# Where x's transposed blocks wait for their store: in the tiles of v's quadrants, in eight pieces, instead of in operand slots

## The chip, the cores and the metric

The kernel runs on one core of one Trainium2 chip. The metric is the device time of one execution in microseconds (us). A core has TensorE (PE, with its weight loads as PEld), VectorE (DVE), ScalarE (ACT), GpSimd (POOL) and SyncE (SP), which issues all DMAs of this kernel. Each engine works through its own queue in order and waits on semaphores for the others.

## What is computed

One decoder block on x of 1024 tokens by 1024 features, in float32. The start, with which this case deals, is a normalization of x, its projection by `w_in`, and beside it the keys and values of a memory of 256 tokens:

```python
h = h + hybrid_mixer(rmsnorm(h, norm_mix[i]), w_in[i], ...)
h = h + mem_cross_attention(rmsnorm(h, norm_xattn[i]), rmsnorm(mem, norm_mem[i]), w_xq[i], w_xkv[i], w_xo[i])
h = h + swiglu(rmsnorm(h, norm_ffn[i]), w_ffn_in[i], w_ffn_out[i])
return rmsnorm(h, norm_final)
```

`hybrid_mixer` projects to z, x/B/C, dt, q, k, v, r, a1 and two gates, runs a state space branch and a gated linear attention branch, and merges them. `mem_cross_attention` takes `k, v = split(m @ w_xkv, 2)`.

## The kernel before

**Products.** A large product is done by a scheme of Strassen's kind: seven half-sized products (`CHAIN`: B11, B21, T1, B22, T2, T3, T4) instead of eight. One factor's seven operands are sums and differences of the blocks of x; `Operands` builds them from `hb`, the normalized, transposed x. To keep float32 precision every operand is split in a high and a low part (`B11h`, `B11l`, ...), and weights likewise (`whi`, `wlo`); each product is three matmuls. The splits are a copy on ScalarE (L223) and a subtraction on VectorE or GpSimd (L73, `either()` picks by a running estimate when the program is built).

**Operand slots.** The pool "op" has 14 slots of 8 KB a partition. Its first users are the memory (`mt`), x (`xt`, four), the weights for keys and values (`raw`, eight in turn), the memory's two halves (`mh`, `ml`), four tiles `xs`, and then the operands, two slots each. A slot is taken again when its user before has been read for the last time.

**The start of the program.** `x_steps()` goes over two halves `j` of the tokens and eight blocks `k` of the features: TensorE transposes a block into a PSUM bank, VectorE scales it into `hb[k]` (named `hs` in the profile), ScalarE copies it unscaled into `xs` (L608), and after four blocks SP stores 1 MB to `xT_d` (L610). `xT_d` is read again only late, for the residual. `kv_unit()` does the memory's keys and values in eight units of 256 columns; each loads 1 MB (`raw`, L513), splits it, does its matmuls and stores the result (`vm_d` or `kT_d`). `v_steps()` computes v by the seven products with 264 columns each (256 of v and 8 of a small projection): the first product goes to the quadrant tile `vq10`, the second to `vq00`, the third to `vq11`, the fourth to `vq01`; `vsa` holds a sum of the weights' quadrants. These tiles are `[P, 4, 264]`, one buffer each. PSUM has four `bank` and four `acc` tiles; both the transposes and the later units of `kv_unit` use `bank`.

**What sets the order.** The program is written as interleaved generators, and a scheduler then orders each engine's queue by readiness and priority; when a tile is free is part of readiness. SP's DMAs go through one queue with eight semaphores in rotation, so each issue also waits for the DMA issued eight before it.

**The constants.** Among SP's loads at about 34 us stand `dcol` (two loads of single elements of 4 bytes), `dtb` and `alog`.

Of the kernel before, what the change touches and what calls it, by code (L numbers as in the profile page):

```python
# [9 lines left out]
F32 = mybir.dt.float32  # L10
F32R = mybir.dt.float32r
I32 = mybir.dt.int32
AF = mybir.ActivationFunctionType
# [3 lines left out]
P = 128  # L17
# [3 lines left out]
HALF = TOK // 2  # L21
# [57 lines left out]
def block_kernel(ctx: ExitStack, tc: tile.TileContext, t: dict, out: bass.AP):  # L79
    nc = tc.nc  # L80
    now = [0.0]
    PE, ACT, SP = Tensor(nc.tensor, now), nc.scalar, nc.sync
# [7 lines left out]
    def pool(name, bufs=1, space=None, stack=None):  # L90
        kw = {"reuse_waits": "tile"} if space is None else {"space": space}
        return (stack or ctx).enter_context(tc.tile_pool(name=name, bufs=bufs, **kw))
# [6 lines left out]
    def dram(name, *shape):  # L99
        return dr.tile(list(shape), F32, name=name, tag=name)  # L100

    xT_d = dram("xT_d", D, TOK)
# [22 lines left out]
    def bank(dt=F32):  # L125
        return ps.tile([P, 512], dt, name="bank", tag="bank", bufs=4)
# [6 lines left out]
    half = lambda j: slice(j * HALF, (j + 1) * HALF)  # L133
# [8 lines left out]
    def slot(key, shape=(P, 2, TOK), dt=F32, name="sl"):  # L142
        pl, n = slots[key]
        return pl.tile(list(shape), dt, name=name, tag="sl", bufs=n)
# [6 lines left out]
    vp = pool("vp", 1, stack=st1)  # L151
# [40 lines left out]
    def col(name, i=0):  # L192
        which, at = gcol[name]
        return cols[:, which, at + i:at + i + 1]
# [12 lines left out]
    def rsqrt(o, v, scale):  # L207

        DVE.tensor_scalar(o, v, scale, EPS, ALU.mult, ALU.add)
        POOL.tensor_tensor(o, o, mhalf[:, :o.shape[1]], ALU.pow)  # L210
# [3 lines left out]
    def spread(p, r, n):  # L214

        for c in range(n):
            d = diag[c % 2]
            DVE.tensor_scalar(d, ident, r[:, c:c + 1], None, ALU.mult)
            PE.matmul(p[:, c * P:(c + 1) * P], ones, d, start=True, stop=True)
# [319 lines left out]
    for k in range(NB):  # L539
        p = bank()  # L540
# [9 lines left out]
    def kv_unit(c0):  # L550
# [32 lines left out]
        else:  # L583
            SP.dma_start(vm_d[:, c0 - D:c0 - D + 256].rearrange("(i p) c -> p i c", p=P), s)

    def x_steps():
        p = bank()
        spread(p, mss, 2)
        DVE.tensor_copy(mbc, p[:, :MEM])
        yield  # L590
        for j in range(2):
            for c in range(4 * j, 4 * j + 4):
                ACT.activation(msq, wide(xt[c // 2][:, c % 2]), AF.Square, accum_out=xr[:, c:c + 1])
            rsqrt(xr[:, 4 * j:4 * j + 4], xr[:, 4 * j:4 * j + 4], 1.0 / D)
            yield
            p = bank()
            spread(p, xr[:, 4 * j:4 * j + 4], 4)
            ACT.activation(rbc[:, half(j)], p, AF.Copy)
            yield
            for k in range(NB):  # L600
                if k % 4 == 0:
                    xs = slot("op", (P, 4, HALF), name="xs")
                p = bank()
                for a in range(4):
                    c = 4 * j + a
                    PE.transpose(p[:, a * P:(a + 1) * P], xt[c // 2][:, c % 2, k * P:(k + 1) * P], ident)
                DVE.scalar_tensor_tensor(hb[k][:, half(j)], p, col("norm_mix", k), rbc[:, half(j)], ALU.mult, ALU.mult)
                ACT.activation(xs[:, k % 4], p, AF.Copy)  # L608
                if k % 4 == 3:
                    SP.dma_start(xT_d[(k - 3) * P:(k + 1) * P, half(j)].rearrange("(k p) s -> p k s", p=P), xs)  # L610
                yield

    B = Operands(hb, 4)
# [4 lines left out]

    dt_t = cp.tile([P, NCH, NH], F32, name="dt_t")
    a1_t = cp.tile([P, NCH, NH], F32, name="a1_t")  # L620
    HW = 264

    vraw = {}

    def load_v(pr):
        if pr not in vraw:
            rr = vraw[pr] = [vp.tile([P, 4, 2 * HW], F32, name="vraw", tag=f"vraw{h}") for h in range(2)]
            for i in range(2):
                v0 = V0 + 512 * pr + 256 * i
                a0 = (DT0, A0)[pr] + 8 * i  # L630
                for h in range(2):
                    for c0, n, o in ((v0, 256, i * HW), (a0, 8, i * HW + 256)):
                        SP.dma_start(rr[h][:, :, o:o + n],
                                     w_in[512 * h:512 * h + 512, c0:c0 + n].rearrange("(k p) c -> p k c", p=P))
        return vraw[pr]

    def v_steps():
        for pr in range(2):
            rr = load_v(pr)
            A11, A21 = rr[0][:, :, :HW], rr[0][:, :, HW:]  # L640
            A12, A22 = rr[1][:, :, :HW], rr[1][:, :, HW:]
            s = {ij: vp.tile([P, 4, HW], F32, name="vq", tag=f"vq{ij[0]}{ij[1]}") for ij in
                 ((0, 0), (0, 1), (1, 0), (1, 1))}
# [6 lines left out]

            sa = vp.tile([P, 4, HW], F32, name="vsa", tag="vsa")
            for n, name in enumerate(CHAIN):
# [42 lines left out]

    kvg = chain(kv_unit(c) for c in kv_cols)
    xg = x_steps()
    load_v(0)
    for n in range(12):
# [681 lines left out]
    for n in range(len(at) + 2):  # L1381
        a = at[n] if n < len(at) else None
        b = at[n - 1] if 0 < n <= len(at) else None
# [208 lines left out]
    for x, (n, k, kn) in enumerate(todo):  # L1592
        name = CHAIN[n]
# [58 lines left out]
```

## Time and profile before

| | |
|---|---|
| median of 3 runs | 2020.72 us (2018.88 to 2021.11) |
| the profiled execution | 2022.57 us |
| its span | 2020.5 us |
| granted TensorE clock, mean | 0.992 |
| TensorE busy | 1953.7 us, 97% |
| VectorE, ScalarE, GpSimd busy | 1313.8, 860.8, 656.3 us |
| DMA | 309.58 MB, 153 GB/s over the span |

Times in the profile are in us from the start of the span. In a list of waits a row names who waits, for whom, the total, the number of waits and the longest. In a timeline a row gives start, duration, engine, line, operation, `out<-in`, tile sizes and count; in brackets at its end stands the idle time before it and what ended that. A matmul's duration overlaps the next one's, so the pace is read from the starts.

### The profile page before, as it was taken

The numbers are of one execution on the slowest core, as the hardware profiler recorded it, in microseconds if no ns is written. First come the engines' busy times: TensorE is split into PE (matmuls) and PEld (weight loads), VectorE is DVE, ScalarE is ACT, GpSimd is POOL, SyncE is SP. The second block draws the span as 40 slices with busy tenths as digits, with TensorE's granted clock in tenths as the row PEclk, the third lists the DMA queues.
The fourth block names the chain that finished last, engine by engine and source line by source line (L and its number), as shares of the span: only waits on it lengthen the run. The fifth ranks groups of instructions, "written<-read, shape, count | busy, mean of one in ns | idle before, by whom it ended". The sixth has DMA issues, their size and how long they took to land.

```text
span 2020.5 us, 26310 instructions
## 1 busy us (share of the span) xinstructions
PE 1953.7 (97%) x9772; PEld 1620.7 (80%) x9772; DVE 1313.8 (65%) x1869; ACT 860.8 (43%) x1482; POOL 656.3 (32%) x480
## 2 busy tenths in 40 slices
PE   7899899999999989999999999999999999999998
PEld 7899678877777777787788888877888888887887
DVE  6856679979886656532454227478777777774565
ACT  7434745465552455432233226453333333354243
POOL 4421243455653212023322100255444444430002
PEclk9899999999999999999999999999999999999999
DMA  7532233356553655797773210433224223276463
GB/s 247 194 117 88 94 124 116 113 181 190 168 173 110 208 163 177 244 357 244 289 237 132 80 42 22 139 124 108 79 89 134 90 82 114 77 259 218 152 227 129
DMA packets 241635, 309.58 MB, mean 153 GB/s; under 512 B 17354, under 2 KB 165044, under 8 KB 241508
## 3 DMA queue, kind: packets, MB, share of 16 engines
q1 hardware_dynamic: 241508, 307.91, 45.2%
q8 instruction: 77, 1.26, 0.3%
q14 instruction: 50, 0.41, 0.1%
HBM read 211.07 MB, written 96.80 MB: 152 GB/s over the span
## 4 chain that ended last, share of the span: by engine, by line
PE 46%; DVE 3%; DMA 2%; issue 1%; POOL 1%; ACT 1%; SPq 0%; POOLq 0%; ACTq 0%; DVEq 0%
PE acc L51 41%; PE bank L51 4%; DMA gates<-gg_d 1%; DMA fr<-act_d 1%; DVE fs L73 1%; PE bank L55 1%; POOL ssum L73 0%; POOL pre L73 0%; DMA pre<-in_w_ffn_out_dram 0%; DMA down_d<-pre 0%; DMA ysg_d<-gates 0%; DVE o L73 0%; DVE wlo L73 0%; DVE T2l L73 0%; DVE T4l L73 0%
## 5 line engine op out<-in xcount | busy, mean ns | idle before, releaser
L51 PE MATMUL acc<-hl,wd 128*128 128x512 f32 x1920 | 443.4, 391 | 6.0 <-DVE wd L73 2.9
L51 PEld LDWEIGHTS acc<-hl,wd 128*128 128x128 f32 x1920 | 360.4, 188 | 84.9 <-DVE wd L73 5.5
L73 DVE TENSOR_TENSOR wlo<-raw,whi 128x512 fp32r<-128x512 f32 x264 | 243.2, 925 | 77.1 <-ACT whi L223 76.8
L223 ACT ACTIVATE whi<-raw 128x512 fp32r<-128x512 f32 x272 | 170.2, 629 | 253.1 <-PE acc L51 224.8
L73 DVE TENSOR_TENSOR o<-acc,o 128x512 f32<-128x512 f32 (+1 forms) x256 | 172.5, 675 | 112.9 <-PE acc L51 100.6
L51 PE MATMUL acc<-fs 128*128 128x512 f32 (+1 forms) x792 | 156.0, 356 | 1.6 <-ACT o L1547 1.5
L51 PEld LDWEIGHTS acc<-fs 128*128 128x128 f32 x792 | 130.6, 189 | 22.7 <-ACT o L1547 1.9
L73 POOL TENSOR_TENSOR raw<-raw,sa 128x512 f32<-128x512 f32 x48 | 65.3, 1361 | 252.8 <-DVE wlo L73 247.1
L223 ACT ACTIVATE fs<-fr 128x1024 fp32r<-128x1024 f32 (+1 forms) x84 | 80.0, 984 | 112.7 <-PE acc L51 38.5
L73 DVE TENSOR_TENSOR fs<-fr,fs 128x1024 fp32r<-128x1024 f32 (+1 forms) x84 | 99.8, 1218 | 38.7 <-ACT fs L223 38.1
L73 DVE TENSOR_TENSOR wd<-raw,wd 128x1024 fp32r<-128x1024 f32 x40 | 50.3, 1260 | 83.1 <-ACT wd L223 82.9
L223 ACT ACTIVATE whi<-sa 128x512 fp32r<-128x512 f32 x96 | 60.0, 626 | 103.5 <-PE acc L51 103.4
L73 POOL TENSOR_TENSOR sa<-raw 128x512 f32<-128x512 f32 x47 | 74.0, 1575 | 86.2 <-DMA raw<-in_w_in_dram 47.7
L73 DVE TENSOR_TENSOR wlo<-sa,whi 128x512 fp32r<-128x512 f32 x96 | 82.6, 861 | 22.8 <-ACT whi L223 21.3
L73 POOL TENSOR_TENSOR raw<-raw 128x512 f32<-128x512 f32 x48 | 81.6, 1702 | 4.9 <-DVE sa L73 4.9
L73 POOL TENSOR_TENSOR ssum<-ssum,sq 128x512 f32<-128x512 f32 (+1 forms) x23 | 35.2, 1531 | 146.9 <-ACT sq L490 143.0
L51 PE MATMUL acc<-B21h,whi 128*128 128x512 f32 x192 | 76.9, 401 | 3.1 <-ACT o L353 3.1
L51 PE MATMUL acc<-T1h,whi 128*128 128x512 f32 x192 | 76.7, 399 | 2.7 <-ACT whi L223 2.7
L73 POOL TENSOR_TENSOR o<-o 128x512 f32<-128x512 f32 x29 | 49.2, 1703 | 91.1 <-DVE o L73 80.8
L51 PE MATMUL acc<-B21h,wlo 128*128 128x512 f32 x192 | 76.3, 398 | 2.5 <-DVE wlo L73 2.5
L51 PE MATMUL acc<-T1h,wlo 128*128 128x512 f32 x192 | 77.4, 403 | 0.5 <-DVE wlo L73 0.5
L51 PE MATMUL acc<-B22h,wlo 128*128 128x512 f32 x192 | 77.5, 404 | 0.0
(375 smaller groups left out, 4801.5 us busy)
## 6 DMA issues: line engine op xcount, KB each, us to landing
raw<-in_w_in_dram SPq DMA_DIRECT2D x26, 1024.0 KB, 5.7
raw<-in_w_ffn_in_dram SPq DMA_DIRECT2D x22, 1024.0 KB, 6.3
act_d<-o SPq DMA_DIRECT2D x77, 256.0 KB, 2.1
fr<-act_d SPq DMA_DIRECT2D x35, 512.0 KB, 6.8
pre<-in_w_ffn_out_dram SPq DMA_DIRECT2D x11, 1024.0 KB, 8.6
fr<-down_d SPq DMA_DIRECT2D x20, 512.0 KB, 3.7
down_d<-pre SPq DMA_DIRECT2D x33, 256.0 KB, 3.4
raw<-in_w_xkv_dram SPq DMA_DIRECT2D x8, 1024.0 KB, 11.4
```

What stands on the lines that cost most here:

```text
L51: return s.e.matmul(o, x, y, **kw)
L55: return s.e.transpose(o, x, i)
L73: return f(*a, **kw)
L223: ACT.activation(hi, src, AF.Copy)
```

## The change

The four tiles `xs` of four blocks leave the pool "op". Each block pair of x is copied into one of the tiles that v uses later (`XS_HOME`: first half vq10, vq00, vq11, vq01; second half vsa, vq00, vq11, vq01) and stored by itself: eight stores of 512 KB instead of four of 1 MB. The tiles vq00, vq11 and vq01 are used twice in turn, and after that all five go to v.

```diff
+    HW = 264
+
+    XS_HOME = ("vq10", "vq00", "vq11", "vq01", "vsa", "vq00", "vq11", "vq01")
+
     def x_steps():
...
             for k in range(NB):
-                if k % 4 == 0:
-                    xs = slot("op", (P, 4, HALF), name="xs")
+                if k % 2 == 0:
+                    xs = vp.tile([P, 4, HW], F32, name="xs", tag=XS_HOME[4 * j + k // 2])
+                    xs = xs.rearrange("p a b -> p (a b)")[:, :2 * HALF].rearrange("p (k s) -> p k s", k=2)
                 p = bank()
...
-                ACT.activation(xs[:, k % 4], p, AF.Copy)
-                if k % 4 == 3:
-                    SP.dma_start(xT_d[(k - 3) * P:(k + 1) * P, half(j)].rearrange("(k p) s -> p k s", p=P), xs)
+                ACT.activation(xs[:, k % 2], p, AF.Copy)
+                if k % 2:
+                    SP.dma_start(xT_d[(k - 1) * P:(k + 1) * P, half(j)].rearrange("(k p) s -> p k s", p=P), xs)
                 yield
```

The instructions on each engine stay the same in number, but for four more stores. Their order differs in the first part of the program, up to the product T1 of v, and in a few swaps of loads much later.

ScalarE before, from the split of B21's high parts on; a wait on `DMAHW` is one for a DMA, here for the store that frees T1h's slot:

```order
L223 ACTIVATE B21h<-hs 128x512 x4
L608 ACTIVATE xs<-bank 128x512 [waits DVE_49]
L223 ACTIVATE T1h<-hs 128x512 [waits DMAHW2_49,Pool_49]
L223 ACTIVATE T1h<-hs 128x512 [waits Pool_49]
L608 ACTIVATE xs<-bank 128x512 [waits DVE_49]
L684 ACTIVATE vq<-acc 128x264 [waits PE_49]
L223 ACTIVATE T1h<-hs 128x512 [waits Pool_49]
L684 ACTIVATE vq<-acc 128x264 [waits PE_49]
L608 ACTIVATE xs<-bank 128x512 [waits DVE_49]
```

ScalarE now, at the same work; the DMA waits here are for the first, second and third piece (and behind these rows comes one for the fourth):

```order
L223 ACTIVATE T1h<-hs 128x512 [waits Pool_49] x2
L687 ACTIVATE vq<-acc 128x264 [waits DMAHW3_49]
L687 ACTIVATE vq<-acc 128x264 x2
L687 ACTIVATE vq<-acc 128x264 [waits PE_49]
L223 ACTIVATE T1h<-hs 128x512 [waits Pool_49]
L613 ACTIVATE xs<-bank 128x512 [waits DMAHW4_49,DVE_49]
L613 ACTIVATE xs<-bank 128x512 [waits DVE_49]
L223 ACTIVATE T1h<-hs 128x512 [waits Pool_49]
L223 ACTIVATE B22h<-hs 128x512 [waits DVE_49,PE_49]
L223 ACTIVATE B22h<-hs 128x512 [waits DVE_49] x2
L613 ACTIVATE xs<-bank 128x512 [waits DMAHW6_49,Activation_49]
L613 ACTIVATE xs<-bank 128x512
```

The wait has moved from T1h to the copies of x and of v's first product, and B11h and B21h stand some rows further ahead.

SP before, from the fourth load of weights for the memory (the first row) to the second store of x:

```order
L513 DMA raw<-in_w_xkv_dram 128x8x256 [waits DMAHW2_49]
L202 DMA dcol<-in_ssd_D_dram 64x8x1 [waits DMAHW3_49]
L202 DMA dcol<-in_ssd_D_dram 64x8x1 [waits DMAHW4_49]
L204 DMA dtb<-in_ssd_dt_bias_dram 128x16 [waits DMAHW5_49]
L205 DMA alog<-in_ssd_A_log_dram 128x16 [waits DMAHW6_49]
L584 DMA vm_d<-kvs 128x2x256 [waits DMAHW7_49,Activation_49]
L584 DMA vm_d<-kvs 128x2x256 [waits DMAHW0_49,Activation_49]
L513 DMA raw<-in_w_xkv_dram 128x8x256 [waits DMAHW1_49]
L610 DMA xT_d<-xs 128x4x512 [waits DMAHW2_49,Activation_49]
L584 DMA vm_d<-kvs 128x2x256 [waits DMAHW3_49,Activation_49]
L610 DMA xT_d<-xs 128x4x512 [waits DMAHW4_49,Activation_49]
```

SP now, from the fifth such load (the fourth stands right ahead of it) to the third piece of x:

```order
L513 DMA raw<-in_w_xkv_dram 128x8x256 [waits DMAHW3_49]
L202 DMA dcol<-in_ssd_D_dram 64x8x1 [waits DMAHW4_49]
L202 DMA dcol<-in_ssd_D_dram 64x8x1 [waits DMAHW5_49]
L204 DMA dtb<-in_ssd_dt_bias_dram 128x16 [waits DMAHW6_49]
L205 DMA alog<-in_ssd_A_log_dram 128x16 [waits DMAHW7_49]
L584 DMA vm_d<-kvs 128x2x256 [waits DMAHW0_49,Activation_49]
L584 DMA vm_d<-kvs 128x2x256 [waits DMAHW1_49,Activation_49]
L513 DMA raw<-in_w_xkv_dram 128x8x256 [waits DMAHW2_49,PE_49]
L615 DMA xT_d<-xs 128x2x512 [waits DMAHW3_49,Activation_49]
L615 DMA xT_d<-xs 128x2x512 [waits DMAHW4_49,Activation_49]
L513 DMA raw<-in_w_xkv_dram 128x8x256 [waits DMAHW5_49,Pool_49]
L615 DMA xT_d<-xs 128x2x512 [waits DMAHW6_49,Activation_49]
```

One more load of `raw` now stands ahead of the constants, and two more (one of them ahead of the first piece) stand between the constants and the third piece.

More of the change, by code (lines that the diff above doesn't have):

```diff
@@ L620, in block_kernel @@
     a1_t = cp.tile([P, NCH, NH], F32, name="a1_t")
-    HW = 264
     vraw = {}
```

## The prediction

> **What bounds the kernel now.** I read the page's busy times and slices first, then windows over the start of the program, the list of waits there, and the timelines of single engines.
>
> ```profile
> span 2020.5 us, 26310 instructions
> PE 1953.7 (97%) x9772; PEld 1620.7 (80%) x9772; DVE 1313.8 (65%) x1869; ACT 860.8 (43%) x1482; POOL 656.3 (32%) x480
> PE   7899899999999989999999999999999999999998
> PEclk9899999999999999999999999999999999999999
> ```
>
> TensorE is busy for 97% of the span. Outside the first slices nothing but its own work sets the end, so a change moves the end by what it moves TensorE's matmul stream at its weak places. The second slice (50 to 101 us) is the only one with a lowered granted clock (8), and the changed stores are issued there. Windows of 10 us (columns: length, then busy us and instructions of PE, PEld, DVE, ACT and POOL, granted clock, DMA share, GB/s):
>
> ```profile
> 40.00:50.00 10.00, 6.80 (x33) 6.50 (x34) 9.76 (x12) 7.91 (x15) 7.41 (x6) 0.68 0.21 58
> 50.00:60.00 10.00, 5.87 (x44) 5.66 (x43) 6.78 (x6) 2.50 (x6) 7.73 (x5) 0.84 1.07 393
> 60.00:70.00 10.00, 6.25 (x27) 5.66 (x27) 9.33 (x8) 3.97 (x9) 7.93 (x5) 0.50 0.99 362
> 70.00:80.00 10.00, 10.00 (x82) 10.00 (x81) 7.85 (x11) 6.56 (x14) 2.13 (x2) 0.95 0.44 136
> 80.00:90.00 10.00, 10.00 (x85) 10.00 (x85) 8.25 (x10) 5.04 (x10) 3.00 (x2) 1.00 0.23 80
> ```
>
> From 40 to 70 us TensorE works 6.80 + 5.87 + 6.25 = 18.9 of 30 us, much of it at half clock; from 70 on it is full. The stretch is a chain of waits (waiting instruction, what released it, us in total, times, longest):
>
> ```profile
> ACT T1h L223 <- DMA xT_d<-xs: 7.6, 1, 7.6
> PE bank L51 <- ACT xs L608: 4.1, 1, 4.1
> DVE T1l L73 <- DMA xT_d<-xs: 3.9, 1, 3.9
> PE bank L51 <- DVE wlo L73: 3.0, 1, 3.0
> ```
>
> ScalarE and VectorE wait for stores of xs, because the operand T1 takes the slots that xs leaves; TensorE waits behind both. The store is late because of the queue ahead of it:
>
> ```profile
> 34.10 2.86 SPq L202 DMA_DIRECT2D dcol<-in_ssd_D_dram  x2
> 38.25 4.16 SPq L584 DMA_DIRECT2D vm_d<-kvs  x2
> 42.47 0.46 SPq L513 DMA_DIRECT2D raw<-in_w_xkv_dram  x1
> 43.02 4.93 SPq L610 DMA_DIRECT2D xT_d<-xs  x1
> 48.04 2.57 SPq L584 DMA_DIRECT2D vm_d<-kvs  x1
> ...
> 40.00:47.00 7.00, 3.80 (x19) 3.50 (x20) 6.76 (x9) 6.53 (x13) 4.41 (x4) 0.76 0.05 3
> 50.00:55.00 5.00, 5.00 (x40) 4.84 (x38) 5.00 (x5) 0.00 (x0) 5.00 (x4) 0.95 1.08 389
> 55.00:60.00 5.00, 0.87 (x5) 0.82 (x5) 1.77 (x2) 2.50 (x6) 2.73 (x2) 0.73 1.06 398
> 60.00:66.00 6.00, 2.25 (x9) 1.66 (x9) 5.33 (x5) 3.33 (x8) 4.56 (x3) 0.50 1.07 390
> ```
>
> The constants dcol (single 4-byte elements) pass at 3 GB/s from 40 to 47 us; then the queue streams full at 389 to 398 GB/s until past 66 us. Stores in that stretch land when the bytes ahead of them have passed.
>
> **The change part by part.** (1) Removed: T1's operands no longer wait for a store; what that is worth is in the walk below, where another wait ends last. (2) Added: an xs copy of the second half must wait until the earlier store from its home has landed (second half's blocks 2-3 on piece 1, 4-5 on piece 2, 6-7 on piece 3), and so must the evacuation of v's first product (on piece 0). They stand in ScalarE's queue, so everything behind them waits too: T1h, B22h, the weight splits for k and v. (3) Moved: B11h and B21h go ahead, v's first product starts earlier, and the fifth `raw` load goes ahead of the constants, which nothing reads before v's products are done. (4) Four more stores of half the size; all other instruction counts stay.
>
> What ends last in the new order is the last product for the memory's v, whose first matmul reuses the bank that the copy of block 5 must leave; that copy waits for piece 2. The rows for it:
>
> ```profile
> 57.49 1.15 ACT L223 ACTIVATE T1h<-hs 128x512 fp32r<-128x512 f32 x2 [7.59 <-DMA xT_d<-xs]
> 58.55 0.58 ACT L608 ACTIVATE xs<-bank 128x512 f32<-128x512 f32 x1
> 70.47 0.64 ACT L223 ACTIVATE whi<-vraw 128x528 fp32r<-128x528 f32 x1 [1.92 <-PE bank L51]
> 54.77 0.28 PE L51 MATMUL acc<-wlo,B11h 128*128 128x264 f32 x1
> 59.18 0.58 PE L51 MATMUL bank<-whi,mh 128*128 128x256 f32 x1 [4.13 <-ACT xs L608]
> 65.37 0.58 PE L51 MATMUL bank<-wlo,mh 128*128 128x256 f32 x1 [3.03 <-DVE wlo L73]
> 71.05 0.28 PE L51 MATMUL bank<-whi,mh 128*128 128x256 f32 x1
> 71.99 0.29 PE L51 MATMUL acc<-whi,B21h 128*128 128x264 f32 x1
> 84.91 0.29 PE L51 MATMUL acc<-whi,T1h 128*128 128x264 f32 x1
> ```
>
> Piece 2's landing. The first 1 MB store is seen landed at 57.49. Between the constants' end and that landing there pass, beside two small stores, one `raw` and one store: 2 MB. In the new order three `raw` (one now ahead of the constants, which pushes them back by its own time) and three pieces of 0.5 MB pass: 4.5 MB. The 2.5 MB more (2.62 million bytes) at 392 GB/s, the mean of the three windows, take 6.7 us: 64.2 us. Two copies of 0.58 follow: the product starts at 65.3, against 59.18 before.
>
> But before, that early start was worth little: after 8 matmuls TensorE stood still for VectorE until 65.37. From there 26 matmuls took 5.68 us (65.37 to 71.05, 0.218 each, the half clock), and from B21's first to T1's first 108 matmuls took 84.91 - 71.99 = 12.92 us (0.1196 each). By the new order 156 matmuls lie between that product's first and T1's first: 26 at the slow rate after the idle time, 130 at the fast one. 65.3 + 5.68 + 15.55 = 86.6, against 84.91: **+1.7 us**. Behind T1 both orders agree until late in the program, and TensorE is full, so what is late here is late at the end.
>
> TensorE: Matmul & The Clock Gate of the Trainium skill (Part 1: The HAM clock gate) says that the clock is full after about 3.4 us of sustained work. The trace shows 5.7 us of slow matmuls, and the measurement decides; by that page of the skill some 16 matmuls would be slow, the other 10 would save 1 us, and the sum would be 1 us less.
>
> Then VectorE. B21's second low half needs a `wlo` split, which stands behind a first one and four B22l: six operations after ScalarE's split of vraw, which itself waits for TensorE to free the weights (70.47 in the row, 5.1 after 65.37; so 70.4 + 0.64 = 71.0). TensorE wants it 82 matmuls after the product's first: 65.3 + 5.68 + 56 x 0.1196 = 77.7. What one operation costs depends on GpSimd:
>
> ```profile
> 60.67 2.98 DVE L73 TENSOR_TENSOR T1l<-hs,T1h 128x512 fp32r<-128x512 f32 x3 [3.90 <-DMA xT_d<-xs]
> 69.21 1.77 DVE L73 TENSOR_TENSOR hs<-hs 128x512 f32<-128x512 f32 x1
> 74.72 1.89 DVE L73 TENSOR_TENSOR B22l<-hs,B22h 128x512 fp32r<-128x512 f32 x3
> 37.67 2.43 POOL L73 TENSOR_TENSOR vsa<-vraw 128x1056 f32<-128x1056 f32 x1 [3.96 <-DMA vraw<-in_w_in_dram]
> 46.40 11.33 POOL L73 TENSOR_TENSOR hs<-hs 128x512 f32<-128x512 f32 x7 [0.63 <-DVE B11l L73]
> 67.08 5.06 POOL L73 TENSOR_TENSOR hs<-hs 128x512 f32<-128x512 f32 x3 [0.63 <-DVE T1l L73]
> ```
>
> With GpSimd idle it is 0.63 (1.89 for three), beside it 1.0 to 1.77. In the new order GpSimd does the last hs differences (1.62 to 1.69 each) after the late transposes and then vsa and its partner (2.43 each), which before were over by about 42.5. Six operations take 3.8 us (ready at 74.8, hidden) to 10.6 us (81.6, a stall of 3.9). A stall in mid-stream can cost up to 10 matmuls of the clock again, 10 x 0.098 = 1.0. The bounds are 0 and 5; I take the middle, **+2.5**. Sum: 1.7 + 2.5 = **+4.2 us** (+1.7 to +6.7).
>
> Edits at nothing: the rest of the new order is swaps among gate, `ga` and `raw` loads in the up-projections:
>
> ```profile
> 930.00:1040.00 110.00, 105.34 (x449) 84.42 (x448) 51.02 (x62) 30.26 (x45) 39.13 (x28) 0.98 0.78 275
> ```
>
> TensorE idles 4.7 of these 110 us; the swaps can move 2 or so either way, and I take 0. The early evacuation of v's product is hidden: 57.49 + (one `raw` and 0.5 MB less than a 1 MB store) puts piece 0 near 59, and nothing needs those banks before B21 at 72.
>
> The profiled execution took 2022.57 us for its span of 2020.5. Its span becomes 2024.7. The median of the runs is 2020.72, 1.85 below that execution; the edit adds the same there: 2020.72 + 4.2 = **2024.9 us**.
>
> **The rivals.** 0.2% is 4.0 us, about what a measurement of this kernel can tell from no change.
>
> B, faster: the early operands pay. TensorE idles 11.1 us of 40 to 70; if pieces 1 and 2 land before they are missed, the product for the memory's v follows v's first product at 54.9 (row 54.77) instead of standing still until 65.37: 10.5 us less, and about 2.5 of the slow clock less (26 x 0.098), minus up to 4 that VectorE's queue then takes: 9 us, 2011.7. It decides for B if piece 2 lands before about 55. For it: the pieces are half as large and ready earlier on ScalarE. Against it: 3 GB/s until 47, and 4.5 MB ahead. 0.19.
>
> C, about the same: the fifth `raw` finds room in the constants' idle queue and pushes nothing; its 1 MB takes 2.7 us off piece 2. 4.2 - 2.7 = 1.5: 2022.2. Against it: the constants pass only after what was issued ahead. 0.08.
>
> D, much slower: GpSimd is busy until past 85, and VectorE does the two hs differences as well before B22l: eight operations of 1.77 from 71.0 end at 85.2, 7.5 after 77.7; with the clock's 1.0 and the 1.7: +10.2, 2030.9. 0.06.
>
> E, each store pays a start of its own, so smaller ones are dearer.
>
> ```profile
> act_d<-o SPq DMA_DIRECT2D x77, 256.0 KB, 2.1
> ```
>
> A lone 256 KB store lands 2.1 us after issue, of which 262 KB at 392 GB/s are 0.7: 1.4 us of start. Three pieces pay it where one store did: +2.8, in all +7.0, 2027.7. Against it: from 57.49 to 60.67 (first and second store seen landed) 1.31 million bytes passed in 3.18 us, 412 GB/s: no room for a start when the queue is full. 0.05. The page DMA: Bandwidth & Descriptors of the Trainium skill (section Bandwidth) asks for transfers of 1 MiB or more, and its fit gives each about 2.0 us of fixed cost, measured from GpSimd's queue; by it the sum would be 4.0 more than mine, not 2.8. The trace of this full queue speaks against it.
>
> **How the numbers follow.** My forecast A has 0.62. Its 1.7 to 6.7 lies more than half beyond 4.0: 0.36 slower, 0.26 within 0.2%. C's 0.08 is within, D and E are slower, B is faster. Slower 0.36 + 0.11 = 0.47, same 0.34, faster 0.19. The range leaves out B alone (0.19) and takes in C with 2 us below for the landing time and D's end: 2019.0 to 2031.0. A's own range is 2022.4 to 2027.4.
>
> **What would show it.** In the changed profile: a wait of xs copies, vq copies or ScalarE for the xT stores of several us; the kv matmuls starting at 65 +/- 1.5, not before 60; slow matmuls for 5.7 us after it; T1's first matmul at 88 to 90; no T1h wait for a store. The forecast is wrong if T1 starts before 85 or TensorE has no idle time between 55 and 65. If VectorE's wlo is in time, T1 starts at 86.6 and the middle of (0, 5) was too much.

## The result and the profile after

The changed kernel takes 2032.39 us (median of 5 runs, 2027.97 to 2033.99) where the kernel before took 2020.72 on the same chip: ratio 1.0054, 95% interval 1.0040 to 1.0068, which is +10.9 us (8.1 to 13.7). The forecast was +4.2, with 2031.0 as the end of its range. Below, "+x us" is always (ratio - 1) x 2020.72 against runs of the kernel before on the same chip, with its interval in brackets.

The page after, its span and busy times:

```profile
span 2029.5 us, 26325 instructions
PE 1955.2 (96%) x9772; PEld 1623.5 (80%) x9772; DVE 1302.8 (64%) x1869; ACT 862.2 (42%) x1482; POOL 652.6 (32%) x480
```

TensorE works 1.5 us longer than before (1955.2 against 1953.7); the other 7.5 of the 9 us more are idle time. The windows over the start (length, busy us and instructions of PE, PEld, DVE, ACT and POOL, granted clock, DMA share, GB/s):

```profile
40.00:50.00 10.00, 6.71 (x56) 6.23 (x54) 9.87 (x16) 5.51 (x10) 5.41 (x4) 1.00 0.33 88
50.00:60.00 10.00, 0.00 (x0) 0.00 (x0) 1.01 (x1) 0.78 (x3) 5.79 (x5) 0.51 0.84 300
60.00:70.00 10.00, 6.17 (x26) 5.54 (x27) 5.31 (x7) 6.71 (x14) 6.00 (x5) 0.50 1.07 369
70.00:80.00 10.00, 8.63 (x66) 8.18 (x65) 7.97 (x6) 4.03 (x7) 7.91 (x4) 0.96 0.48 173
```

The timelines of ScalarE and TensorE there:

```profile
59.22 1.24 ACT L687 ACTIVATE vq<-acc 128x264 f32<-128x264 f32 x4 [11.45 <-DMA xT_d<-xs]
63.52 1.67 ACT L223 ACTIVATE B22h<-hs 128x512 fp32r<-128x512 f32 x3 [1.05 <-PE bank L55]
65.09 1.07 ACT L613 ACTIVATE xs<-bank 128x512 f32<-128x512 f32 x2
67.39 1.08 ACT L613 ACTIVATE xs<-bank 128x512 f32<-128x512 f32 x2 [0.71 <-DMA xT_d<-xs]
...
61.51 1.97 PE L55 MATMUL bank<-ident,xt 128*128 128x128 f32 x8 [14.54 <-ACT xs L613]
66.21 0.58 PE L51 MATMUL bank<-whi,mh 128*128 128x256 f32 x1
75.73 0.39 PE L51 MATMUL acc<-wlo,B21h 128*128 128x264 f32 x1 [0.52 <-DVE wlo L73]
81.02 0.39 PE L51 MATMUL acc<-wlo,B21h 128*128 128x264 f32 x1 [1.86 <-DVE wlo L73]
89.89 0.29 PE L51 MATMUL acc<-whi,T1h 128*128 128x264 f32 x1
```

ScalarE stands 11.45 us at v's first evacuation until piece 0 has landed; the copies of x stand behind it, keep their banks, and TensorE stops for 14.54 us. T1 starts at 89.89 instead of 84.91: 4.98 us late. That is the forecast loss. A second one stands much later, in the up-projections. The window 1010 to 1020 us, first before, then after:

```profile
1010.00:1020.00 10.00, 10.00 (x45) 8.28 (x45) 5.99 (x7) 3.26 (x5) 5.62 (x4) 1.00 0.57 197
```

```profile
1010.00:1020.00 10.00, 3.87 (x10) 2.39 (x9) 3.12 (x4) 2.62 (x4) 0.00 (x0) 0.64 0.66 246
```

Some names first: `pre` is 1 MB of the weights `w_ffn_out`, from which GpSimd and VectorE make sums (`sa`, and again `pre`) that SP stores to `down_d`. `gates` are values that ScalarE turns into gates. `raw` is here 1 MB of weights of the up-projections, and `wd` is its split, the weights of TensorE's matmuls.

What led there in the changed kernel, by the timelines of SP (start, length of the issue), GpSimd, ScalarE and TensorE:

```profile
990.17 0.32 SPq L1256 DMA_DIRECT2D gates<-gg_d  x1
990.91 0.38 SPq L1227 DMA_DIRECT2D pre<-in_w_ffn_out_dram  x1
...
1000.65 0.32 SPq L1231 DMA_DIRECT2D down_d<-sa  x1
...
1004.47 0.38 SPq L1143 DMA_DIRECT2D raw<-in_w_o_dram  x1
1004.96 0.73 SPq L1256 DMA_DIRECT2D gates<-gg_d  x1
...
998.78 1.85 POOL L73 TENSOR_TENSOR sa<-pre 128x512 f32<-128x512 f32 x1 [10.11 <-DMA pre<-in_w_ffn_out_dram]
...
1014.24 1.15 ACT L1260 ACTIVATE gates<-gates 128x512 f32<-128x512 f32 x2 [10.70 <-DMA gates<-gg_d]
1015.30 1.04 ACT L223 ACTIVATE wd<-raw 128x1024 fp32r<-128x1024 f32 x1
...
1016.39 43.95 PE L51 MATMUL acc<-hl,wd 128*128 128x512 f32 x178 [6.09 <-ACT wd L223]
```

The same steps in the kernel before:

```profile
987.96 0.38 SPq L1224 DMA_DIRECT2D pre<-in_w_ffn_out_dram  x1
988.70 0.32 SPq L1253 DMA_DIRECT2D gates<-gg_d  x1
...
994.41 0.32 SPq L1228 DMA_DIRECT2D down_d<-sa  x1
...
999.62 0.43 SPq L1140 DMA_DIRECT2D raw<-in_w_o_dram  x1
1000.15 0.65 SPq L1253 DMA_DIRECT2D gates<-gg_d  x1
...
993.09 1.29 POOL L73 TENSOR_TENSOR sa<-pre 128x512 f32<-128x512 f32 x1 [8.12 <-issue]
...
1006.54 1.15 ACT L1257 ACTIVATE gates<-gates 128x512 f32<-128x512 f32 x2 [4.77 <-DMA gates<-gg_d]
```

Counted through both traces, TensorE reaches the same matmul at 986.87 us before and at 987.04 after, so these times compare directly. `pre` is now issued behind `gates`. GpSimd's sum starts 7.9 us after that issue instead of 5.1; the store of the sum waits at the head of SP's queue, and `raw` and the next `gates` behind it go out 4.8 us later than before. ScalarE gets that gate 7.7 us later (it comes 9.3 us after its issue instead of 6.4; why stays open), the weight split `wd` stands behind it, and TensorE waits 6.09 us for `wd`.

The stop costs more than its length, and it follows a smaller gain. From 1000 to 1030 us TensorE starts 136 matmuls before and 95 after (the granted clock is 0.64 and then 0.85 in the two windows from 1010). But from 980 to 1000 us it starts 71 before and 86 after, since a stop of 2.01 us that the kernel before has at 986.87 is missing in the changed one.

So the theory: two separate losses, the start by the forecast walk, and the up-projections by the new order of the loads. The rival: one loss, the start's, and the stop at 1010 only shows it again.

### The profile page after: what moved, and what is told of

Same layout as the page of the kernel before. It is cut to its first block, busy times and chain, and to the rows that moved or that the text cites. A ratio compares the mean times of both kernels' runs of the same rounds, so it can differ in the third digit from the quotient of the medians.

```text
span 2029.5 us, 26325 instructions
## 1 busy us (share of the span) xinstructions
PE 1955.2 (96%) x9772; PEld 1623.5 (80%) x9772; DVE 1302.8 (64%) x1869; ACT 862.2 (42%) x1482; POOL 652.6 (32%) x480
## 4 chain that ended last, share of the span: by engine, by line
PE 48%; DMA 5%; DVE 3%; issue 3%; ACT 2%; POOL 1%; SPq 0%; POOLq 0%; ACTq 0%; DVEq 0%
PE acc L51 43%; PE bank L51 5%; DMA gates<-gg_d 1%; DMA gates<-gs_d 1%; PE bank L55 1%; DMA pre<-in_w_ffn_out_dram 1%; DMA fr<-act_d 1%; DVE fs L73 1%; DMA ysg_d<-gates 0%; DMA down_d<-pre 0%; POOL ssum L73 0%; DMA hl<-ys_d 0%; ACT gates L1260 0%; DVE gates L73 0%; POOL pre L73 0%
## 5 line engine op out<-in xcount | busy, mean ns | idle before, releaser
L73 DVE TENSOR_TENSOR wlo<-raw,whi 128x512 fp32r<-128x512 f32 x264 | 238.8, 908 | 79.5 <-ACT whi L223 79.3
L73 DVE TENSOR_TENSOR wd<-raw,wd 128x1024 fp32r<-128x1024 f32 x40 | 51.5, 1289 | 89.1 <-ACT wd L223 88.8
L51 PE MATMUL acc<-B22h,whi 128*128 128x512 f32 x192 | 76.2, 397 | 1.4 <-ACT whi L223 1.4
```

The source lines that it names most:

```text
L51: return s.e.matmul(o, x, y, **kw)
L73: return f(*a, **kw)
```

## The experiments

**The late order by itself.** In these kernels the order of SP's DMAs and ScalarE's activations from the middle of the program to the up-projections' end is written out, with edges that set the order of issue and add no wait. TensorE's progress through the up-projections is read from one window, 930 to 1060 us: the fewer of its matmuls fall into it, the more was lost there. Before:

```profile
930.00:1060.00 130.00, 125.34 (x537) 100.98 (x536) 59.06 (x72) 37.15 (x55) 42.32 (x30) 0.99 0.76 265
...
1050.00:1080.00 30.00, 30.00 (x134) 24.86 (x133) 11.53 (x15) 10.33 (x15) 8.98 (x6) 1.00 0.48 158
```

At full pace 134 matmuls take 30 us, 0.224 each. The old late order gives 537 here, 539 in e1 and 546 in e5 (both below), so the count is good to some 9 matmuls, 2 us. The changed kernel has 506, 31 less, so about 6.9 us are lost here:

```profile
930.00:1060.00 130.00, 120.58 (x506) 97.30 (x505) 54.97 (x69) 34.87 (x52) 39.35 (x30) 0.95 0.74 262
```

e1, the changed kernel with the late order of the kernel before:

```diff
+    pin(mybir.EngineType.SP, "DMA", SP_BACK)                  # ranks as in the kernel before
+    pin(mybir.EngineType.Activation, "Activation", ACT_BACK)
```

> The changed kernel with one thing undone: in the up-projections SP's DMAs and ScalarE's instructions are held in the order that they have in the kernel before (edges that only set the order of issue, no waits). The start of the program is that of the change. Theory A (the late order costs most): T1 starts at 89 to 91 as in the changed kernel, the stall near 1010 us is gone, and the start's 5 us are mostly taken up by waits that come anyway before 950 us; 2020 to 2024 us. Theory B (the start's delay is carried to the end and the rest is chance): about 2025 to 2027 us. Theory C (the late order does nothing): 2032 us.

Measured: 2024.74 us, ratio 1.0018 (1.0008 to 1.0028), +3.6 us (1.6 to 5.7). T1 starts at 88.26, the stop at 1010 is gone, and the window is as full as before:

```profile
930.00:1060.00 130.00, 125.12 (x539) 100.96 (x538) 58.16 (x72) 37.15 (x55) 42.22 (x30) 0.99 0.75 261
```

e2, the kernel before with the late order of the changed kernel (the same two lines with its ranks):

> The kernel before with one thing added: the up-projections' DMAs and ScalarE's instructions in the order that they have in the changed kernel. xs stays in the operand slots. Theory A: the start is that of before (T1 at 85), a stall of 5 to 6 us and the slow clock near 1005 us; 2027 to 2031 us. Theory B: at most 2026 to 2027 us. Theory C: 2020 to 2022 us.

Measured: 2027.62 us, 1.0030 (1.0017 to 1.0043), +6.1 us (3.4 to 8.7). The stop is there without the change at the start:

```profile
1012.26 24.68 PE L51 MATMUL acc<-hl,wd 128*128 128x512 f32 x98 [5.71 <-ACT wd L223]
```

3.6 + 6.1 = 9.7, which agrees with 10.9 within the intervals. These are two losses that add: each stands without the other, so the rival falls.

**Which part of the late order.** e7 tried ScalarE: the changed kernel with each weight split ahead of the gate activations that it stands behind; e8 did the same to e5 (below).

```diff
-ACT: gates<-gates x2, wd<-raw
+ACT: wd<-raw, gates<-gates x2
```

> The changed kernel with its own late order of DMAs, and on ScalarE in the up-projections each split of the next weights (wd) put ahead of the pair of gate activations that stands before it. Theory: the stall at 1010 us is the split of wd behind a wait for a gate's load; it goes, and the time is 2022 to 2026 us, near that of the first run. Rival (the late load of raw or the acc banks are the limit): 2029 to 2033 us.

> The kernel before with both: the dense dcol and wd ahead of the gates. Theory: TensorE's 4.7 us of idle time and the slow clock between 930 and 1040 us go too: 3 to 5 us less than with the dense dcol alone, 2009 to 2015 us. Rival: a gate that is late frees its acc bank late, and the time is that of the dense dcol alone or more.

Measured: e7 2037.62 us, 1.0082 (1.0068 to 1.0095), +16.6; e8 2026.99 us, 1.0026 (1.0016 to 1.0036), 9.5 above e5. Both the wrong way. In e7 TensorE still waits for a split:

```profile
1006.21 23.96 PE L51 MATMUL acc<-hl,wd 128*128 128x512 f32 x96 [6.20 <-ACT wd L223]
```

Putting every split first is no cure: what waits is then something else. (e8 loses nothing between 930 and 1060, 546 matmuls, as e5. It loses ahead of that: from 870 to 930 us it starts 233 matmuls and e5 268, 7.8 us at 0.224 each. TensorE waits there 3.24 us at 892.90 for a gate on VectorE and 2.02 us at 917.98 for a split.)

e9 and e10 each make one move in SP's order of the changed kernel, e13 both:

```diff
 SP: ga<-ysg_d
+SP: pre<-in_w_ffn_out          # e9, e13
 SP: gates<-gg_d
-SP: pre<-in_w_ffn_out          # e9, e13
 SP: ga<-ysg_d
+SP: raw<-in_w_o, gates<-gg_d   # e10, e13
 SP: down_d<-sa, down_d<-pre, ga<-ysg_d, down_d<-pre
-SP: raw<-in_w_o, gates<-gg_d   # e10, e13
```

> The changed kernel with its own late order written out, and one swap in it: in the up-projections the load of pre (the row at about 991 us) is issued ahead of the load of gates that stands right before it, as in the kernel before. Theory: this one swap makes the second loss. The late pre makes GpSimd's sum late, the sums' stores down_d wait at the head of SP's queue, and the raw and the gate behind them are issued 5 to 6 us late. Then the stop of 6.1 us at 1010 us is gone and the time is that of the changed kernel with the old late order, 2024.7 (2023 to 2028). Rival: the stop comes from the other swaps, or from several together, or it only moves to the next gate: 2029 to 2034, with as much idle time of TensorE between 985 and 1040.

> The changed kernel with its own late order written out, and one move in it: the load of raw and the load of gates behind it are issued ahead of the two down_d stores and two ga loads before which they had to wait; pre stays late. Theory: what costs is the wait of the stores at the head of SP's queue, so raw and gate come in time even with a late pre, the stop at 1010 is gone: 2023 to 2028. Rival: pre itself is what is missed (its sum or its store feeds what comes next), or the bytes moved ahead make something else late: 2029 to 2034.

> The changed kernel with its own late order written out, and both moves of the two kernels before together: pre ahead of gates, and raw and gates ahead of the two down_d stores. Each alone took away the stop of 6.1 us at 1010 and gave 2.5 to 3 us, with other stops of 2 to 2.3 us in its place. If the two are separate terms, they add: 2025 to 2028. If any early transfer makes another one late, so that the sum of the stops is what the whole order leaves, the two give no more than one: 2029 to 2033, with stops of 2 us at other places between 930 and 1060.

Measured: e9 2030.06 us, 1.0034 (1.0021 to 1.0047), +6.9; e10 2029.78 us, 1.0035 (1.0023 to 1.0047), +7.1; e13 2033.18 us, 1.0050 (1.0035 to 1.0065), +10.1. In e9 and e10 the stop of 6.09 us is gone, but only about 4 of the late 7 us come back, and together the two give nothing. e9's timeline of TensorE:

```profile
1000.50 0.73 PE L51 MATMUL acc<-hl,wd 128*128 128x512 f32 x2 [2.17 <-ACT wd L223]
1003.25 56.91 PE L51 MATMUL acc<-hl,wd 128*128 128x512 f32 x239 [2.02 <-DVE wd L73]
```

And e13's, with its window:

```profile
1001.69 1.22 PE L51 MATMUL acc<-hl,wd 128*128 128x512 f32 x2 [2.42 <-ACT wd L223]
1004.45 34.18 PE L51 MATMUL acc<-hl,wd 128*128 128x512 f32 x142 [1.54 <-DVE wd L73]
1040.94 0.73 PE L51 MATMUL acc<-hl,wd 128*128 128x512 f32 x2 [2.31 <-ACT wd L223]
...
930.00:1060.00 130.00, 120.69 (x508) 97.23 (x507) 53.75 (x68) 33.58 (x50) 37.15 (x29) 0.96 0.74 257
```

One long stop became several of about 2 us. I read it so that a load that is moved forward makes a neighbour late; these rows show the new stops, not which load made them.

So the last three kernels change one engine's order as a whole. All are the changed kernel; e15 has SP's new and ScalarE's old late order, e16 SP's old and ScalarE's new, and e14 ScalarE's old and SP's new one but for `pre` ahead of `gates` (as e9), one `raw` a row earlier and a few `down_d` stores a row earlier.

```diff
-    SP new, ScalarE new      # the changed kernel
+    SP new, ScalarE old      # e15
+    SP old, ScalarE new      # e16
+    SP new with pre ahead of gates, ScalarE old   # e14
```

> The changed kernel with ScalarE's order in the up-projections as in the kernel before; SP's order then comes out as in the changed kernel, but for pre ahead of gates (as in e9) and the one raw load one row earlier. Against e9 (2030.1) this takes ScalarE's order alone. If the other half of the late loss is that a weight split wd stands behind a later gate on ScalarE, the time is that of the old late order, 2023 to 2027. If it lies in SP's order, 2029 to 2033.

> The changed kernel; in the up-projections SP keeps the new order and ScalarE gets the old one. With e1 (both old, +3.6 over the kernel before) and the changed kernel (both new, +10.9) it makes a table of two by two. If the loss lies in SP's order: 2030 to 2034, and the stop near 1010 stays. If it lies in ScalarE's order, where a weight split wd stands behind one more gate: 2023 to 2027. If each carries half: 2027 to 2030.

> The changed kernel; in the up-projections SP gets the old order and ScalarE keeps the new one, the fourth cell of the table. If the loss lies in SP's order: 2023 to 2027. If it lies in ScalarE's: 2030 to 2034. If each carries half: 2027 to 2030. If the two together make the loss (a late load matters only where a split stands behind its gate): both this one and e15 are at 2023 to 2027.

Measured: e14 2027.70 us, 1.0021 (1.0010 to 1.0032), e15 2031.04, 1.0043 (1.0026 to 1.0060), e16 2027.52, 1.0028 (1.0017 to 1.0040). As a table, over the kernel before:

| | ScalarE old | ScalarE new |
|---|---|---|
| SP old | +3.6 (e1) | +5.7 (3.4 to 8.1) (e16) |
| SP new | +8.7 (5.3 to 12.1) (e15) | +10.9 (the changed kernel) |

By both columns SP's order costs 5.1 to 5.2 us, by both rows ScalarE's 2.1 to 2.2; each cell is uncertain by 2 to 3.4, so the split is rough. e14 has +4.2 (2.0 to 6.5) where e15 has +8.7: with ScalarE's order old, its moves in SP's order take back 4.5 of SP's 5.1. `pre` ahead of `gates` is one of them and was not taken alone here, and the two intervals overlap. The windows of e15, e16 and e14 go the same way (509, 522 and 526 matmuls, so 6.3, 3.4 and 2.5 us lost by 537, each good to 2 us):

```profile
930.00:1060.00 130.00, 121.04 (x509) 96.64 (x508) 54.84 (x69) 34.94 (x52) 40.59 (x30) 0.97 0.74 259
```

```profile
930.00:1060.00 130.00, 122.73 (x522) 98.81 (x521) 57.13 (x69) 35.08 (x53) 41.77 (x31) 0.97 0.78 266
```

```profile
930.00:1060.00 130.00, 122.58 (x526) 98.59 (x525) 54.02 (x69) 34.96 (x52) 42.95 (x33) 0.99 0.77 267
```

In e15 ScalarE waits as long for that gate as in the changed kernel, and TensorE stops at 1014.80 for 1.11 us only:

```profile
1012.65 1.15 ACT L1260 ACTIVATE gates<-gates 128x512 f32<-128x512 f32 x2 [10.63 <-DMA gates<-gg_d]
...
989.25 0.73 PE L51 MATMUL acc<-hl,wd 128*128 128x512 f32 x2 [1.82 <-ACT wd L223]
...
1014.80 0.73 PE L51 MATMUL acc<-hl,wd 128*128 128x512 f32 x2 [1.11 <-ACT wd L223]
```

Yet it loses nearly the same time, in shorter stops around it. As I read it, the late loads are the cost, and ScalarE's order decides in which stops it shows; which load costs how much was not taken further apart.

**The start.** e3 moves the constants (`dcol`, `dtb`, `alog`) behind v's third store, in the changed kernel with the old late order; e4 does so in the kernel before.

```diff
-    late_constants()
+    with tc.issue_after(stored[2]):
+        late_constants()
```

> The changed kernel with the late order of before, as in the first run, and the loads of dcol, dtb and alog issued behind v's third store instead of at 36 us. If the constants' pause holds up the pieces of x, they land some 7 us earlier, the kv matmuls start at 58 to 60 and T1 at 81 to 84; the end then lies 1 to 6 us below the first run's, by how much of an early start later waits take up: 2015 to 2021 us. If the bytes ahead of the pieces hold them up and not the pause, T1 starts at 88 to 90 and the time is the first run's.

> The kernel before with the same move of the constants and its own late order held. If the pause is what holds up the stores of x, the waits of T1h and T1l for them shrink from 7.6 and 3.9 us to near 0, T1 starts at 77 to 81, and the time is 2014 to 2019 us. If not, 2020 to 2022 us.

Measured: e3 2033.34 us, 1.0056 (1.0037 to 1.0075), +11.3; e4 2031.97 us, 1.0048 (1.0032 to 1.0064), +9.7. In e3 the early stretch gains as meant (the memory's product starts at 56.40 instead of 64.58 in e1), but the pause goes along with the constants. At 135 us the queue moves 1 GB/s, v's store behind them is late, and TensorE stands 8.29 us:

```profile
145.97 0.59 PE L51 MATMUL acc<-whi,B21h 128*128 128x264 f32 x1 [8.29 <-ACT vq L690]
...
135.00:140.00 5.00, 2.67 (x23) 2.46 (x21) 0.00 (x0) 0.00 (x0) 3.28 (x3) 1.00 0.05 1
```

e4 has the same stop there (8.77 us at 145.59). So e5 and e6 take the pause away: `dcol` is read as 16 dense values for each partition, and GpSimd spreads them after v's products; `dtb` and `alog` stay. e5 is the kernel before, e6 the changed kernel with the old late order.

```diff
-        for a in range(2):
-            SP.dma_start(dcol[a * 64:(a + 1) * 64, :],
-                          t["ssd_D"].rearrange("(j a) -> a j", a=2)[a].partition_broadcast(64))
+        dall = cp.tile([P, 2 * NB], F32, name="dall")
+        SP.dma_start(dall, t["ssd_D"].partition_broadcast(P))
+        with tc.issue_after(counted[1]):
+            for a in range(2):
+                r = slice(a * 64, (a + 1) * 64)
+                nc.gpsimd.tensor_copy(dcol[r, :], dall[r].rearrange("p (j a) -> p a j", a=2)[:, a])
```

> The kernel before with dcol's two loads of single elements replaced by one load of 16 contiguous values to every partition, as dtb and alog are loaded, and two small copies on GpSimd behind the v products; all other orders are those of before. Theory: the pause of 40 to 47 us is dcol's elements; it shrinks to 2 us or less, the stores of x land 5 to 6 us earlier, T1 starts at 78 to 82 and the time is 2013 to 2018 us. Rival: later waits take the early start up again, 2019 to 2021 us.

> The same dense load of dcol in the changed kernel, with the late order of before held (the first run of the first set, but for dcol). Theory: piece 2 lands near 56, the kv matmuls start at 56 to 58 and T1 at 81 to 84; against the run above 2 to 4 us more, since two more raw loads still stand ahead of the pieces: 2016 to 2021 us. Rival (the change costs only by the pause): the same time as the run above.

Measured: e5 2017.45 us, 0.9979 (0.9967 to 0.9991), -4.2 us (-6.7 to -1.8): the fastest of all, and faster than both kernels. e6 2018.94 us, 0.9990 (0.9978 to 1.0001). The queue moves 332 GB/s where it had stood at 3, and in e5 the next wait is VectorE's split:

```profile
40.00:47.00 7.00, 5.65 (x35) 4.80 (x35) 6.04 (x9) 6.37 (x13) 3.21 (x3) 0.77 0.98 332
...
62.79 0.58 PE L51 MATMUL bank<-wlo,mh 128*128 128x256 f32 x1 [6.38 <-DVE wlo L73]
```

With the pause gone the changed start looks 2.2 us slower than the old one by the ratios (e6 over e5), 1.5 by the medians; the intervals overlap, so this is not clear of noise. In e6 TensorE still waits 8.6 us for ScalarE's copies of x (e5: 0.3), and then for VectorE's `wlo`:

```profile
73.40 0.39 PE L51 MATMUL acc<-wlo,B21h 128*128 128x264 f32 x1 [4.10 <-DVE wlo L73]
```

e11 adds to e5 the move of e10:

> The kernel before with dcol as one dense load (2017.4 when it was run alone) and with raw and gates issued ahead of the same two down_d stores. Theory: the kernel before has a small stop of the same kind (a gate's wait of 4.8 us on ScalarE near 1006, TensorE idle 4.7 us in 930 to 1040), so it gains 0 to 3: 2014.5 to 2017.5. Rival: a gate that comes earlier takes a place on ScalarE or in the memory's queue that other work needed, as when the weight splits were put first: 2019 or more.

Measured: 2023.90 us, 1.0006 (0.9996 to 1.0017), by the ratios 5.4 us slower than e5 (the two ran on different chips): the rival. The old order too is spoilt by one move.

e12 is the kernel before with stores of half the size:

```diff
-                if k % 4 == 3:
-                    SP.dma_start(xT_d[(k - 3) * P:(k + 1) * P, half(j)].rearrange("(k p) s -> p k s", p=P), xs)
+                if k % 2:
+                    SP.dma_start(xT_d[(k - 1) * P:(k + 1) * P, half(j)].rearrange("(k p) s -> p k s", p=P),
+                                 xs[:, k % 4 - 1:k % 4 + 1])
```

> The kernel before, with x stored in eight pieces of two blocks but still from the two operand slots; the late order is the old one. It takes the size of the stores alone. By my account a store pays nothing for its start in a full queue: 2019 to 2022, and T1's first matmul at 84 to 86. Rival E: each further store pays 1.4 us of start on the way to T1: T1 later by 1.4 to 2.8, the time 2022 to 2024.

Measured: 2023.00 us, 1.0005 (0.9995 to 1.0015), +1.0 us (-1.0 to 3.0); T1 starts at 86.38, 1.47 later. By itself this does not decide it: two executions with the same start order, e1 and the changed kernel, have T1 at 88.26 and 89.89. By e12's interval a cost of the size up to 3 us stays open; the landings below say more.

## Why the prediction was wrong

**The start: right in its path, with two loose pieces.** Piece 2 was to land at 64.2, and the landings in the changed kernel's trace have it at 64.41. The memory's product was to start at 65.3 and did at 66.21; piece 0 was to land near 59, and ScalarE's wait for it ended at 59.22; T1 was to start at 89.1 (84.91 + 4.2) and did at 89.89. In the nine executions with this start T1 begins between 88.26 and 89.89. Alone, with the old late order, the start costs +3.6 (1.6 to 5.7). About 0.7 us of the product's 0.9 come from what the prediction called hidden: behind the wait for piece 0 ScalarE was still at three splits B22h when piece 2 landed, so the copies of blocks 4 and 5 began at 65.09 and not at 64.41.

VectorE's stall was the first loose piece. It was taken as 2.5 and was 0.52 + 1.86 = 2.4, but 2.5 was the middle of bounds 0 and 5, so that it fits is luck in part. (65.3 + 5.68 + 15.55 is 86.5, not 86.6 as the prediction has it; nothing hangs on the 0.1.) The 1.0 us of lowered clock in the upper bound, for which the prediction shows no row, did not come: the granted clock is 1.00 from 80 to 90.

The clock after the long stop was the second: 0.50 until 70 and 0.96 in the next 10 us, so about 0.8 us at half speed there and full from about 70.8, 4.6 us after the product's first matmul. That lies between the 3.4 us that TensorE: Matmul & The Clock Gate of the Trainium skill (Part 1: The HAM clock gate) states and the 5.7 that I used.

**"What is late here is late at the end": for the most part.** At 714 us the kernel before waits 1.89 us for ScalarE, the changed one doesn't, and is there 2.1 us late instead of 4.98. Before, then after:

```profile
713.68 0.81 PE L55 MATMUL bank<-ident,o 128*128 128x128 f32 x4 [1.89 <-ACT o L1062]
```

```profile
715.76 0.60 PE L55 MATMUL bank<-ident,o 128*128 128x128 f32 x4
```

But that stop is no part of the change: e2, which has the start of the kernel before, is without it too, and e5 and e12, which are made from the kernel before as well, wait there 1.11 and 0.19 us. So about 2 us of this catching up belong to one execution of the kernel before, which was 1.85 us above its median. By the medians e1, with T1 3.35 us late, ends 3.6 us late.

**The step that failed:** "TensorE idles 4.7 of these 110 us; the swaps can move 2 or so either way, and I take 0." Measured alone they cost +6.1 (3.4 to 8.7), about 5 by SP's order and 2 by ScalarE's. TensorE's idle time bounds what a better order can give; it says nothing of what a worse one can take. The profile before did show the risk: ScalarE waits for this gate already (4.77 us for the one at 1006.54), so it has no time in hand when the gate is issued later, and the weight split stands behind it. And the rows were not only swaps among gate, `ga` and `raw` loads, as the prediction has it. In the two traces SP's order differs at 37 places between 901 and 1028 us; in the kernel before, 14 of them are `down_d` stores and 4 are loads of `pre`. ScalarE's splits `wd` and gate activations change places, too. In the changed kernel `pre` behind `gates` holds GpSimd's sum, the sum's store holds the queue, and the queue holds the next two loads. How the 5 us divide among these rows stays open.

**The rivals.** B fell: piece 2 did not land early, and 50 to 60 us was TensorE's emptiest stretch. C fell with T1 at 89.89, D with it (it wanted 95). E is left open up to 3 us by e12, but the landings speak against it: piece 1 is there 1.09 us after piece 0 (60.29 and 59.20), less than a start of 1.4 and the bytes, and piece 2 at 64.41, where E wanted 64.2 + 2.8 = 67.0. The 4.0 more that the prediction works out by DMA: Bandwidth & Descriptors of the Trainium skill (section Anatomy of one DMA — SWDGE (gpsimd) path), 2.0 for each of two more stores, lies outside e12's interval; 2.0 for one would lie inside. None of the rivals was the second loss.

## What to carry to other kernels

A change at one place of a scheduled program can reorder loads far away: compare the whole order, and price each reordered load by who waits for its consumer, above all a load that goes behind another on a queue whose next entry is a store that waits for that load's result. TensorE's idle and slow time in a stage bounds the gain from a reorder, not the loss. Where the cause is a whole order, single moves mislead (two that each gave 4 us gave nothing together); give each engine its old and new order in turn.

## What was not expected of the hardware

The constants hold the whole DMA queue at 3 GB/s from 40 to 47 us, and it was no better in the other place that was measured: moved some 90 us on, they held the queue at 1 GB/s from 135 to 140 us and v's store with it, and TensorE stood for 8.29 us. The two loads of `dcol` with single elements of 4 bytes do it: read densely, with two copies on GpSimd, and with `dtb` and `alog` left as they were, they let 332 GB/s through from 40 to 47 us, and the kernel is 4.2 us faster (1.8 to 6.7).
